# Last down block cut into 512, 448 and 128 tokens, its outputs on two queues, and two reorderings inside a streaming encoder layer

## The chip, the cores and the metric

The kernel runs on one core of one Trainium2 chip. The metric is the device time of one execution in microseconds (us). Before the change three runs took 1772.66 us in the median, from 1772.01 to 1775.33.

## The reference, cut to what matters

One encoder layer is applied to 1024 new tokens (the prompt) and to 64 tokens of a running stream (the sample), 1088 tokens of width 1024 in all. In short:

```
h = RMSNorm(x) @ W_in                      # one projection for four mixers
x = x + concat[Conv, ForgettingAttn, HGRN2, StickBreaking] @ W_out
x = x + MemoryCrossAttn(RMSNorm(x))        # 4 heads, 256 memory tokens
h = RMSNorm(x)
x = x + square(relu(h @ W_up)) @ W_down    # 1024 -> 4096 -> 1024
y = RMSNorm(x)                             # y_prompt (1024 rows), y_sample (64 rows)
```

Beside y the layer returns the new caches. Two of them are the last 30 inputs of the depthwise convolution, for the prompt and for the sample (conv_p, conv_s, each 30 x 256). Everything is float32 and must come out nearly that exact.

## The kernel before, in words

Activations lie transposed, channels on the 128 partitions and tokens along the free axis, in eight tiles of 128 channels. The tokens are in two groups (GR, L216): 512, and 576 of which the last 64 are the sample. Every dense product is made from three: each operand is split into a high half that the fast matmul takes without loss and a low rest (`split`, L169: ScalarE copies the high half, VectorE subtracts), and high x high, high x low and low x high are added up in PSUM (`mul`, L1270; `mm3`, L188). In the names of the profile `wh`, `wl` are the halves of weights, `ap`, `aq`, `fz`, `xt`, `hx` those of activations; `pw` is one PSUM bank (2 in turn), `pz` two banks (3 pairs in turn).

The program is written as a sequence of tiles and operations. A scheduler puts the operations of each engine in one fixed order ahead of time; it takes what is ready by its plan, the lower `tc.cur_priority` first. The number grows as the program is written down, and the code moves it by hand at some places. At run time each engine goes through its list in order and waits at an operation whose inputs or buffers aren't there.

Three places matter here.

First the end of the convolution (`lane_conv`, L758). It runs as one of four lanes whose work is interleaved. 31 taps for two channel tiles are VectorE's (L794). After the taps of the last chunk the two conv outputs are made (L798 to L805): for each, two transposes of 30 columns into a PSUM bank (`pco`; the pool `ps_cv` has one buffer), a copy by VectorE to `cvo` (its tag `c0` has one buffer too) and a store by SyncE (SP). The next user of `ps_cv` is the sum over channels `pme` (L811), the next of `c0` is `rs`. All lanes come ahead of the dense block of W_out that follows.

Second the first Strassen step of the up projection (loop from L1367, i = 1). The product of W_up with h is made for 2 x 2 blocks with seven products instead of eight. `forms` (L1302) makes the combinations of activations that these need: for each of four k, T1 and T2 (L1305 to L1310) and then T3 and T4 (L1311 to L1313), with their splits. It is called at L1375 inside i = 1, after 800 has been added to the priority (that stays added). `sums` (L1328) makes the combinations of weights, `wform` and `split` their halves (L1377 to L1382). TensorE then takes, for i = 1: W from the first weights (`pa`), Y from S4 and B22, Z from S2 and T2, X from S1 and T1, then onto Z again S3 with T3 and A22 with T4. The tiles wh and wl have two buffers each; those of the second weights (`pb`, S4 and A22) are the ones that the products of i = 0 used.

Third the end. The down projection goes over 8 blocks of 512 hidden channels. In the last (L1496) all weights are split first, and then the tokens are taken in parts of 512, 320 and 256: for each part and each of eight output tiles m twelve matmuls into a `pw` bank and an addition to x by VectorE (L1344, `plus`), and after the eight the part is finished:

```
def finish(g, c0, n):                  # for each 128 tokens of the part
    ps = banks()                       # 2 PSUM banks, one for each half of 1024 channels
    for kb in range(2):
        4 transposes into ps[:, kb]    # TensorE, L1467
        Square with a row sum          # ScalarE, through L74
    1/sqrt of the mean square          # six small steps of VectorE and ScalarE
    for kb: scale by it and by the gain, store   # VectorE L1472, SP L1476 or L1478
```

The last tile of tokens holds 64 rows of the prompt and 64 of the sample, so it has four stores; the others have two.

Of the kernel before, what the change touches and what calls it, by code (L numbers as in the profile page):

```python
# [8 lines left out]
F32 = mybir.dt.float32  # L9
# [3 lines left out]
AF = mybir.ActivationFunctionType  # L13
# [4 lines left out]
P = 128  # L18
D = 1024
KD = D // P  # L20
SP = 1024
# [3 lines left out]
G = 256  # L25
# [27 lines left out]
def kernel(ctx: ExitStack, tc: tile.TileContext, *args):  # L53
    nc = tc.nc
# [8 lines left out]
    y_p, y_s = y_p[0], y_s[0]  # L63
# [9 lines left out]
    def act(out, in_, func, **kw):  # L73
        nc.scalar.activation(out=out, in_=in_, func=func, **kw)  # L74

    V, Q = nc.vector, nc.gpsimd
# [4 lines left out]
    ident = const.tile([P, P], F32, name="ident")  # L81
# [28 lines left out]
    for m in LEVELS[1:]:  # L110
        nb = 64 // m
        f = const.tile([P, nb], F32, name=f"lf{m}", tag="lvlf", bufs=1)
# [56 lines left out]
    def split(hi, lo, src):  # L169
        act(hi, src, AF.Copy)  # L170
        V.tensor_tensor(out=lo, in0=src, in1=hi.bitcast(F32), op=ALU.subtract)  # L171
# [70 lines left out]
    wk = mx.enter_context(tc.tile_pool(name="wk", bufs=2))  # L242
    rb = wk.tile([P, T], F32, name="rb", tag="rb", bufs=1)
    with ExitStack() as pa:
        xa = pa.enter_context(tc.tile_pool(name="xa", bufs=1))
        ps_a = pa.enter_context(tc.tile_pool(name="ps_a", bufs=4, space=PSUM))
        ss = xa.tile([P, 9], F32, name="ss")
# [3 lines left out]
        for i, (t0, n) in enumerate(TT):  # L251
# [3 lines left out]
            if i in (3, 6):  # L255
                c = (C_SK, C_SV)[i // 3 - 1]
# [19 lines left out]
        for c0, cn in CH:  # L276
            tiles = [i for i, (t0, n) in enumerate(TT) if c0 <= t0 < c0 + cn]
            for k in range(KD):
                px = ps_a.tile([P, 512], F32, name="px", tag="px")
                for i in tiles:  # L280
                    t0, n = TT[i]
# [18 lines left out]
    ps_cv = mx.enter_context(tc.tile_pool(name="ps_cv", bufs=1, space=PSUM))  # L300
# [437 lines left out]
    HW = CW - 1  # L738
    CN = 376
    CE = SP - 2 * CN + HW + SS  # L740

    def ct_(name, tag, n=CN):
        return hc.tile([P, n], F32, name=name, tag=tag)
# [6 lines left out]
    ps = ps_cv.tile([P, 4, 64], F32, name="pcw", tag="cv")  # L750
# [7 lines left out]
    def lane_conv():  # L758
        tails = [None, None]
        for t0, np_ in ((0, CN), (CN, CN), (2 * CN, SP - 2 * CN)):  # L760
            last = t0 + np_ == SP
            n, nt = (CE, np_ + SS) if last else (np_, np_)
            ys, exts = [], []
# [32 lines left out]
                if j % 3 == 2:  # L796
                    yield 0.3 + n / 150.0
            if last:  # L798
                for at, dst in ((np_, conv_p), (CE, conv_s)):
                    ps = ps_cv.tile([P, G], F32, name="pco", tag="cv")  # L800
                    for ct in range(2):
                        nc.tensor.transpose(ps[:HW, ct * P:(ct + 1) * P], exts[ct][:, at:at + HW], ident)
                    ot = ct_("cvo", "c0")
                    V.tensor_copy(out=ot[:HW, :G], in_=ps[:HW])
                    nc.sync.dma_start(out=dst[0, 0], in_=ot[:HW, :G])  # L805
            rs = ct_("rs", "c0").rearrange("p (j n) -> p j n", j=2)
            sqs = [ct_(f"sq{ct}", f"ce{ct}", CN + HW) for ct in range(2)]
            for p0, pn in ((0, n // 2), (n // 2, n - n // 2)):
# [12 lines left out]
                v, r, t = rs[:, 0], sq[0], rs[:, 1]  # L821
# [219 lines left out]
    n = GR[0][1]  # L1041
# [222 lines left out]
    def banks():  # L1264
        return psm.tile([P, 2, 512], F32, name="pz", tag="z", bufs=3)
# [36 lines left out]
    def forms(k):  # L1302

        (h11, h12), (h21, h22) = ((xw[0][i], xw[1][i]) for i in (k, k + 4))
        V.tensor_tensor(out=h11[:, :N1], in0=h12[:, :N1], in1=h11[:, :N1], op=ALU.subtract)  # L1305
        act(h11[:, N1:], h12[:, N1:], AF.Copy)
        split(*hb[T1][k], h11)
        V.tensor_tensor(out=h12, in0=h22, in1=h12, op=ALU.subtract)
        V.tensor_tensor(out=h22, in0=h22, in1=h11, op=ALU.subtract)
        split(*hb[T2][k], h22)  # L1310
        split(*hb[T3][k], h12)  # L1311
        V.tensor_tensor(out=h21[:, :N1], in0=h21[:, :N1], in1=h22[:, :N1], op=ALU.subtract)
        split(hb[T4][k][0][:, :N1], hb[T4][k][1][:, :N1], h21[:, :N1])  # L1313
# [53 lines left out]
    for i in range(1, NU):  # L1367
        r1 = fetch_w(w_up, 0, KD, 2 * i * P)
        r2 = fetch_w(w_up, 0, KD, (2 * i + 1) * P)
        pa, pb = ([wp.tile([P, KD, P], F32R, name=nm, tag=nm) for nm in ("wh", "wl")] for _ in range(2))  # L1370
        split(*pa, r1)
        if i == 1:
            tc.cur_priority += 800
            for k in range(4):
                forms(k)  # L1375
        s1 = fz.tile([P, 4, P], F32, name="s1", tag="s1", bufs=1)
        sums(r1[:, :4], r1[:, 4:], r2[:, :4], r2[:, 4:], s1, V)  # L1377
        S2, S1 = wform(r1[:, :4]), wform(s1)
        S3 = wform(r2[:, :4])
        S4, A22 = [t[:, :4] for t in pb], [t[:, 4:] for t in pb]  # L1380
        split(*S4, r1[:, 4:])
        split(*A22, r2[:, 4:])  # L1382
        t1 = t1s[i % 2]
        W, Z, X = bank(), banks(), banks()
        mul(W, [t[:, :4] for t in pa], hb[B11], True, slice(0, N1))
        act(t1[:, :N1], W, AF.Copy)
        c12, c22 = unit("ap"), unit("ap")
        if i == 1:

            mul(W, [t[:, 4:] for t in pa], hb[B21], False, slice(0, N1))  # L1390
            Y = banks()
            mul2(Y, S4, hb[B22], True)
            plus(halves(c12), halves(t1), Y[:, :, :HN])
        mul2(Z, S2, hb[T2], True)
        plus(halves(c12), halves(c12 if i == 1 else t1), Z[:, :, :HN])
        mul2(X, S1, hb[T1], True)
        plus(halves(c22), halves(t1), X[:, :, :HN])
        if i == 1:
            plus(halves(c12), halves(c12), X[:, :, :HN])
        else:  # L1400
            mul(W, [t[:, 4:] for t in pa], hb[B21], False, slice(0, N1))
        c11 = unit("xt")
        square(c11[:, :N1], W)
        mul2(Z, S3, hb[T3], False)
        plus(halves(c22), halves(c22), Z[:, :, :HN])
        square(c22, c22, q)
        if i > 1:
            mul2(X, S4, hb[B22], False)
            plus(halves(c12), halves(c12), X[:, :, :HN])
        square(c12, c12, q)  # L1410
        mul2(Z, A22, hb[T4], False, N1)
        c21 = unit("xt")
        plus(c21[:, :HN], t1[:, :HN], Z[:, 0, :HN])
        plus(c21[:, HN:N1], t1[:, HN:N1], Z[:, 1, :N1 - HN])
        square(c21[:, :N1], c21[:, :N1])
        store_hidden(i, (c11, c12, c21, c22))
# [39 lines left out]
    def finish(g, c0, n):  # L1456

        for i in range(0, n, P):
            w = min(P, n - i)
            t = GR[g][0] + c0 + i  # L1460
            np_ = max(0, min(w, SP - t))
            ss = fs.tile([P, 2], F32, name="fss", tag="fss")
            ps = banks()
            yt = [unit("aq") for _ in range(2)]
            for kb in range(2):
                for k in range(4):
                    nc.tensor.transpose(ps[:w, kb, k * P:(k + 1) * P], xT[g][4 * kb + k][:, c0 + i:c0 + i + w], ident)  # L1467
                act(yt[kb][:w, :512], ps[:w, kb], AF.Square, accum_out=ss[:w, kb:kb + 1])
            V.tensor_tensor(out=ss[:w, 0:1], in0=ss[:w, 0:1], in1=ss[:w, 1:2], op=ALU.add)
            r = rstd_chain(fs, 1, ss[:w, 0:1], "rf", scale=1.0 / D, parts=w)  # L1470
            for kb in range(2):
                V.scalar_tensor_tensor(out=yt[kb][:w, :512], in0=ps[:w, kb], scalar=r, in1=gf[kb][:w],  # L1472
                                       op0=ALU.mult, op1=ALU.mult)
                ys = slice(kb * 512, (kb + 1) * 512)
                if np_:
                    nc.sync.dma_start(out=y_p[t:t + np_, ys], in_=yt[kb][:np_, :512])  # L1476
                if np_ < w:
                    nc.sync.dma_start(out=y_s[t + np_ - SP:t + w - SP, ys], in_=yt[kb][np_:w, :512])  # L1478

    for c in range(NC):  # L1480
        hid = hidden(c)
        if c == 0:
            for k in range(KD):
                for g, (t0, n, _) in enumerate(GR):
                    nc.sync.dma_start(out=xT[g][k], in_=x2_d[k][:, t0:t0 + n])
        if c < NC - 1:
            for j in range(KD // 2):
                for m, w in enumerate(down_w(c, j, None)):
                    ps = bank()
                    mul(ps, w, [hid[k][0] for k in range(NF)], True, slice(0, N1))  # L1490
                    plus(xT[0][2 * j + m], xT[0][2 * j + m], ps)
                    ps = banks()
                    mul2(ps, w, [hid[k][1] for k in range(NF)], True)
                    x = halves(xT[1][2 * j + m])
                    plus(x, x, ps[:, :, :HN])
        else:  # L1496

            ws = []
            for j in range(KD // 2):
                dst = [[t[:, :NF * P].rearrange("p (k c) -> p k c", k=NF) for t in pair(1 - c % 2)] for m in range(2)]  # L1500
                ws += down_w(c, j, dst)
            for g, c0, n in ((0, 0, 512), (1, 0, 320), (1, 320, 256)):
                for m in range(KD):
                    ps = bank()[:, :n]
                    mul(ps, ws[m], [hid[k][g] for k in range(NF)], True, slice(c0, c0 + n))
                    x = xT[g][m][:, c0:c0 + n]
                    plus(x, x, ps)
                finish(g, c0, n)
# [33 lines left out]
```

## Time and profile before

| | |
|---|---|
| runs before, median of 3 | 1772.66 us (1772.01 to 1775.33) |
| profiled execution | 1772.62 us, its span 1770.6 us, mean granted TensorE clock 0.987 |
| TensorE matmul (PE) busy | 1698.2 us, 96% |
| weight load (PEld) busy | 1506.6 us, 85% |
| VectorE (DVE) busy | 1174.6 us, 66% |
| ScalarE (ACT) busy | 791.5 us, 45% |
| GpSimd (POOL) busy | 93.6 us, 5% |

Shares are means over the whole span. A busy TensorE is not yet one at its peak, since matmuls overlap. All dense products stand at line L71, all ScalarE operations at L74 and the low halves of all splits at L171, since helpers record them; they are told apart by the names of the tiles.

### The profile page before, as it was taken

To read this page: it belongs to the slowest core of one execution; us is meant where nothing else is said; L and a number is where in the kernel's file an instruction comes from. 1 tells how busy PE (TensorE), PEld (TensorE's weight loads), DVE (VectorE), ACT (ScalarE), POOL (GpSimd) and SP (SyncE) were. 2 spreads that over 40 slices of the span, in tenths; PEclk is the share of its full clock that TensorE was granted. 3 is DMA by queue.
4 is the path that set the end of the run, shared out by engine and by line. 5 is a ranking of instruction groups with operands and counts; after the bars stand their busy time and mean duration, and the time that the engine had idled before them with its cause. 6 is when DMAs were issued, how large, how long until landed. Compare 5 with 4: busy or idle time off the path is not lost.

```text
span 1770.6 us, 29390 instructions
## 1 busy us (share of the span) xinstructions
PE 1698.2 (96%) x11379; PEld 1506.6 (85%) x11379; DVE 1174.6 (66%) x2231; ACT 791.5 (45%) x1614; POOL 93.6 (5%) x201
## 2 busy tenths in 40 slices
PE   6999999999999979999999989999999999999997
PEld 4987768788777768988899979999999999999987
DVE  6366789988986897668777795555555444444435
ACT  5266657647356755346456353343334212122213
POOL 3021201101020100000000000000000000000000
PEclk9999999999999989999999999999999999999999
DMA  8521322243237357222522323333335732332112
GB/s 255 144 76 44 111 78 84 80 113 88 63 99 215 101 155 233 81 88 68 158 78 72 118 91 107 99 99 103 101 100 194 272 98 87 98 99 73 36 36 102
DMA packets 233195, 194.70 MB, mean 110 GB/s; under 512 B 17502, under 2 KB 199711, under 8 KB 233055
## 3 DMA queue, kind: packets, MB, share of 16 engines
q1 hardware_dynamic: 232799, 192.80, 35.5%
q8 instruction: 90, 1.47, 0.4%
q14 instruction: 50, 0.41, 0.1%
q0 software_dynamic: 256, 0.01, 0.0%
HBM read 137.96 MB, written 53.72 MB: 108 GB/s over the span
## 4 chain that ended last, share of the span: by engine, by line
PE 78%; DVE 13%; ACT 4%; DMA 2%; issue 2%; POOL 0%; SPq 0%; DVEq 0%; POOLq 0%; ACTq 0%
PE pz L71 25%; PE pw L71 16%; PE pm L71 11%; PE pa L71 9%; PE pq L71 5%; PE z L71 2%; DVE y L794 2%; PE pmo L71 2%; PE pms L71 1%; PE po L71 1%; PE pt L517 1%; PE pv L71 1%; DVE hsc L933 1%; DVE sba L494 1%; DVE wl L171 1%
## 5 line engine op out<-in xcount | busy, mean ns | idle before, releaser
L74 ACT ACTIVATE wh<-wr 128x1024 fp32r<-128x1024 f32 (+1 forms) x179 | 161.5, 910 | 446.6 <-PE pz L71 193.8
L171 DVE TENSOR_TENSOR wl<-wr,wh 128x1024 fp32r<-128x1024 f32 (+1 forms) x179 | 184.5, 1037 | 68.8 <-ACT wh L74 67.6
L71 PE MATMUL pw<-ap,wh 128*128 128x512 f32 x720 | 223.4, 391 | 1.3 <-ACT t L74 0.7
L71 PE MATMUL pz<-ap,wh 128*128 128x288 f32 x988 | 198.3, 294 | 0.0
L71 PE MATMUL pa<-ap,wh 128*128 128x256 f32 (+2 forms) x768 | 187.1, 332 | 2.2 <-DVE xt L1119 2.2
L71 PE MATMUL pm<-hx,wh 128*128 128x512 f32 (+1 forms) x640 | 176.4, 364 | 1.9 <-ACT wh L74 1.7
L71 PEld LDWEIGHTS pz<-ap,wh 128*128 128x128 f32 x988 | 161.3, 188 | 4.7
L71 PE MATMUL pm<-ap,wh 128*128 128x256 f32 (+1 forms) x768 | 164.7, 308 | 0.0
L71 PEld LDWEIGHTS pw<-ap,wh 128*128 128x128 f32 x720 | 130.1, 188 | 24.1 <-ACT t L74 1.1
L71 PE MATMUL pz<-ap,wl 128*128 128x288 f32 x494 | 145.5, 294 | 0.0
L71 PEld LDWEIGHTS pa<-ap,wh 128*128 128x128 f32 x768 | 131.7, 190 | 12.6 <-DVE xt L1119 2.4
L71 PE MATMUL pw<-ap,wl 128*128 128x512 f32 x360 | 140.4, 390 | 0.0
L71 PE MATMUL pa<-ap,wl 128*128 128x512 f32 (+2 forms) x384 | 126.8, 331 | 1.1 <-DVE wl L171 1.1
L71 PEld LDWEIGHTS pm<-hx,wh 128*128 128x128 f32 x640 | 110.5, 192 | 20.3 <-ACT wh L74 2.5
L71 PEld LDWEIGHTS pm<-ap,wh 128*128 128x128 f32 x768 | 123.9, 191 | 4.2 <-issue 1.7
L1344 DVE TENSOR_TENSOR xt<-xt,pz 128x576 f32<-128x576 f32 x56 | 42.2, 754 | 113.8 <-PE pz L71 108.5
L71 PE MATMUL pm<-ap,wl 128*128 128x256 f32 (+1 forms) x384 | 114.2, 297 | 0.0
L71 PE MATMUL pm<-hx,wl 128*128 128x512 f32 (+1 forms) x320 | 112.9, 353 | 0.3 <-DVE wl L171 0.2
L794 DVE SCALAR_TENSOR_TENSOR y<-ext,cwT,y 128x376 f32<-128x376 f32 (+1 forms) x180 | 101.1, 609 | 0.3
L1344 DVE TENSOR_TENSOR xt<-xt,pw 128x512 f32<-128x512 f32 (+2 forms) x80 | 51.1, 639 | 69.6 <-PE pw L71 69.6
L71 PE MATMUL pq<-ap,wh 128*128 128x512 f32 (+2 forms) x384 | 93.1, 332 | 0.0
L71 PEld LDWEIGHTS pz<-ap,wl 128*128 128x128 f32 x494 | 92.7, 188 | 0.0
(380 smaller groups left out, 3580.7 us busy)
## 6 DMA issues: line engine op xcount, KB each, us to landing
wr<-in_w_up_dram SPq DMA_DIRECT2D x32, 512.0 KB, 4.0
wr<-in_w_down_dram SPq DMA_DIRECT2D x32, 512.0 KB, 3.5
wr<-in_w_in_dram SPq DMA_DIRECT2D x24, 512.0 KB, 4.3
hid_d<-ap SPq DMA_DIRECT2D x32, 288.0 KB, 2.5
aq<-hid_d SPq DMA_DIRECT2D x32, 288.0 KB, 3.2
wr<-in_w_out_dram SPq DMA_DIRECT2D x16, 512.0 KB, 3.5
wr<-in_w_mq_dram SPq DMA_DIRECT2D x16, 512.0 KB, 3.7
wr<-in_w_mo_dram SPq DMA_DIRECT2D x32, 256.0 KB, 2.7
```

The costliest lines, as they stand in the source:

```text
L71: nc.tensor.matmul(out, lhsT=lhsT, rhs=rhs, start=start, stop=stop, **kw)
L74: nc.scalar.activation(out=out, in_=in_, func=func, **kw)
L171: V.tensor_tensor(out=lo, in0=src, in1=hi.bitcast(F32), op=ALU.subtract)
L494: V.tensor_tensor_scan(out=v[:, ::-1], data0=z[:, n - 1:0:-1], data1=v[:, ::-1], initial=-NEG, op0=ALU.add, op1=ALU.subtract)
L517: nc.tensor.transpose(ps[:w, j - jb], p[:, j * P:j * P + w], ident)
L794: V.scalar_tensor_tensor(out=y, in0=ext[:, j:j + n], scalar=cwT[:, ct, j:j + 1], in1=y, op0=ALU.mult, op1=ALU.add)
L933: V.copy_predicated(sc[r, s_at:s_at + ng, :, r].rearrange("p g h (c w) -> p (g h) c w", w=2 * m)[:, :, :, m:], lvl[m][r, par * nb:(par + 1 ...
L1344: eng.tensor_tensor(out=out, in0=a, in1=b, op=ALU.add)
```

## The change

The conv outputs get one PSUM tile with room for both. All four transposes come first, then one copy of 512 columns into a tile of another pool (tag `nat`, two buffers), then the two stores.

`forms` is cut in two, T1 and T2 in the first, T3 and T4 in the second (`forms2`). The call, with the 800 on the priority, moves behind the sums and splits of the weights of i = 1, and runs the first for all four k and then the second for all four.

In the last block the parts are 512, 448 and 128 tokens. For the part of 128 the two halves of the channels are transposed into two pairs of banks, of which each uses one bank; the other parts keep one pair. The stores of y_sample go out from ScalarE's queue.

```diff
             if last:
-                for at, dst in ((np_, conv_p), (CE, conv_s)):
-                    ps = ps_cv.tile([P, G], F32, name="pco", tag="cv")
+                ps = ps_cv.tile([P, 2, G], F32, name="pco", tag="cv")
+                for o, at in enumerate((np_, CE)):
                     for ct in range(2):
-                        nc.tensor.transpose(ps[:HW, ct * P:(ct + 1) * P], exts[ct][:, at:at + HW], ident)
-                    ot = ct_("cvo", "c0")
-                    V.tensor_copy(out=ot[:HW, :G], in_=ps[:HW])
-                    nc.sync.dma_start(out=dst[0, 0], in_=ot[:HW, :G])
+                        nc.tensor.transpose(ps[:HW, o, ct * P:(ct + 1) * P], exts[ct][:, at:at + HW], ident)
+                ot = wk.tile([P, 512], F32, name="cvo", tag="nat").rearrange("p (o c) -> p o c", o=2)
+                V.tensor_copy(out=ot[:HW], in_=ps[:HW])
+                for o, dst in enumerate((conv_p, conv_s)):
+                    nc.sync.dma_start(out=dst[0, 0], in_=ot[:HW, o])
...
         split(*hb[T2][k], h22)
+
+    def forms2(k):
+
+        (h11, h12), (h21, h22) = ((xw[0][i], xw[1][i]) for i in (k, k + 4))
         split(*hb[T3][k], h12)
...
         split(*pa, r1)
-        if i == 1:
-            tc.cur_priority += 800
-            for k in range(4):
-                forms(k)
         s1 = fz.tile([P, 4, P], F32, name="s1", tag="s1", bufs=1)
         sums(r1[:, :4], r1[:, 4:], r2[:, :4], r2[:, 4:], s1, V)
...
         split(*A22, r2[:, 4:])
+        if i == 1:
+            tc.cur_priority += 800
+            for f in (forms, forms2):
+                for k in range(4):
+                    f(k)
...
-            ps = banks()
+            if n > P:
+                ps = banks()
+                ps = [ps[:, kb] for kb in range(2)]
+            else:
+                ps = [banks()[:, 0] for kb in range(2)]
...
                 if np_ < w:
-                    nc.sync.dma_start(out=y_s[t + np_ - SP:t + w - SP, ys], in_=yt[kb][np_:w, :512])
+                    nc.scalar.dma_start(out=y_s[t + np_ - SP:t + w - SP, ys], in_=yt[kb][np_:w, :512])
...
-            for g, c0, n in ((0, 0, 512), (1, 0, 320), (1, 320, 256)):
+            for g, c0, n in ((0, 0, 512), (1, 0, 448), (1, 448, 128)):
```

## Rows read from the trace of the kernel before

**Rows 1.** Busy us of each engine (x instructions) by stretch, granted clock, DMA.

```profile
640.00:657.40 17.40, 6.76 (x63) 5.11 (x61) 17.40 (x35) 5.01 (x10) 0.00 (x0) 0.76 0.41 133
...
1020.00:1046.00 26.00, 25.36 (x153) 22.94 (x152) 25.93 (x42) 15.54 (x26) 0.00 (x0) 1.00 0.30 96
1046.00:1058.30 12.30, 5.84 (x25) 4.16 (x23) 12.26 (x21) 8.37 (x16) 0.00 (x0) 0.88 0.12 45
1058.30:1073.10 14.80, 14.74 (x96) 14.39 (x97) 9.91 (x15) 3.46 (x6) 0.00 (x0) 0.87 0.27 72
...
1743.70:1758.30 14.60, 14.60 (x123) 14.14 (x122) 9.07 (x29) 5.58 (x20) 0.00 (x0) 1.00 0.27 91
1758.30:1770.60 12.30, 1.73 (x13) 1.05 (x10) 4.73 (x15) 2.65 (x10) 0.00 (x0) 0.65 0.30 85
```

**Rows 2.** Timeline of TensorE around i = 1: start, length, operation [wait, releaser].

```profile
1045.92 0.62 PE L71 MATMUL pw<-ap,wh 128*128 128x512 f32 x2
...
1058.31 0.85 PE L71 MATMUL pz<-fz,wh 128*128 128x288 f32 x2 [5.78 <-ACT wh L74]
...
1062.49 0.43 PE L71 MATMUL pz<-fz,wh 128*128 128x288 f32 x2
...
1062.89 0.43 PE L71 MATMUL pz<-fz,wh 128*128 128x288 f32 x2
```

**Rows 3.** Timeline of VectorE and ScalarE from 1055 us.

```profile
1055.10 0.69 DVE L171 TENSOR_TENSOR xt<-xt 128x512 fp32r<-128x512 f32 x1
...
1056.90 0.69 DVE L1333 TENSOR_TENSOR wr<-wr 128x512 f32<-128x512 f32 x1
...
1057.63 0.63 ACT L74 ACTIVATE wh<-wr 128x512 fp32r<-128x512 f32 x1
...
1059.31 0.69 DVE L171 TENSOR_TENSOR ap<-wr,ap 128x512 fp32r<-128x512 f32 x1
```

**Rows 4.** VectorE's groups by shape, 1026 to 1060 us: busy us, mean ns.

```profile
L1312 DVE TENSOR_TENSOR xt<-xt 128x512 f32<-128x512 f32 x4 | 2.8, 690 | 0.0
L171 DVE TENSOR_TENSOR xt<-xt 128x576 fp32r<-128x576 f32 x3 | 2.3, 755 | 0.0
...
L171 DVE TENSOR_TENSOR xt<-xt 128x512 fp32r<-128x512 f32 x3 | 2.1, 691 | 0.0
```

**Rows 5.** Timeline at the end of the convolution.

```profile
655.68 0.61 PE L802 MATMUL pco<-ident,ext 128*30 128x128 f32 x2 [8.62 <-DVE cvo L804]
...
657.42 0.80 PE L71 MATMUL pa<-ap,wl 128*128 128x512 f32 x1 [1.12 <-DVE wl L171]
...
660.57 1.42 PE L71 MATMUL pme<-y,ones 128*128 128x183 f32 x4
```

**Rows 6.** The chain that ended last, in the last block: start, length, what.

```profile
1703.05 21.89 PE pw L71 x96
...
1736.66 7.08 PE pw L71 x48
...
1755.44 2.88 PE pw L71 x24
```

**Rows 7.** Timeline of TensorE at matmuls of 64 columns.

```profile
941.42 0.28 PE L71 MATMUL pmo<-pT,vl 128*128 128x64 f32 x1
...
942.31 0.28 PE L71 MATMUL pmo<-pT,vl 128*128 128x64 f32 x1
```

**Rows 8.** Timeline of the last two tiles of tokens.

```profile
1758.83 0.31 PEld L1467 LDWEIGHTS pz<-ident,xt 128*128 128x128 f32 x3 [0.20 <-DVE xt L1344]
...
1760.51 0.66 PE L1467 MATMUL pz<-ident,xt 128*128 128x128 f32 x4 [1.14 <-ACT aq L74]
...
1761.47 1.41 DVE L1472 SCALAR_TENSOR_TENSOR aq<-pz,rsy,gf 128x512 f32<-128x512 f32 x2
...
1764.28 1.41 DVE L1472 SCALAR_TENSOR_TENSOR aq<-pz,rsy,gf 128x512 f32<-128x512 f32 x2
...
1766.87 0.59 SPq L1478 DMA_DIRECT2D out_dram<-aq  x1
```

More of the change, by code (lines that the diff above doesn't have):

```diff
@@ L1466, in finish @@
                 for k in range(4):
-                    nc.tensor.transpose(ps[:w, kb, k * P:(k + 1) * P], xT[g][4 * kb + k][:, c0 + i:c0 + i + w], ident)
-                act(yt[kb][:w, :512], ps[:w, kb], AF.Square, accum_out=ss[:w, kb:kb + 1])
+                    nc.tensor.transpose(ps[kb][:w, k * P:(k + 1) * P], xT[g][4 * kb + k][:, c0 + i:c0 + i + w], ident)
+                act(yt[kb][:w, :512], ps[kb][:w], AF.Square, accum_out=ss[:w, kb:kb + 1])
             V.tensor_tensor(out=ss[:w, 0:1], in0=ss[:w, 0:1], in1=ss[:w, 1:2], op=ALU.add)
@@ L1471, in finish @@
             for kb in range(2):
-                V.scalar_tensor_tensor(out=yt[kb][:w, :512], in0=ps[:w, kb], scalar=r, in1=gf[kb][:w],
+                V.scalar_tensor_tensor(out=yt[kb][:w, :512], in0=ps[kb][:w], scalar=r, in1=gf[kb][:w],
                                        op0=ALU.mult, op1=ALU.mult)
```

## The prediction

> **What bounds the kernel now.** I read the stretches first [rows 1]. TensorE is the bound almost everywhere, and it stands idle in three places that the diff touches. Between 640 and 657.4 us it is busy 6.76 of 17.40 us while VectorE is busy for all 17.40. Between 1046 and 1058.3 us it is busy 5.84 of 12.30 us, VectorE 12.26. After 1758.3 us only 1.73 of 12.30 us are left to it: the tail of the last tiles. In both holes VectorE is the engine that ends last; in the tail it is a chain from one token tile to the next. TensorE's clock pays for the holes: it is granted 0.76 in the first, 0.88 in the second and 0.87 in the stretch behind it, and 1.00 where the products flow.
>
> Then the timeline at the second hole [rows 2]. W begins at 1045.92, its last product ends near 1052.3 us, and the product Y (S4 times B22, matmuls pz<-fz,wh) starts at 1058.31 after 5.78 us of waiting for ACT wh, the high half of S4. The other two engines say why [rows 3]: ScalarE writes this wh at 1057.63, directly behind VectorE's L1333 (the last step of `sums`), and that stands at 1056.90 because the whole of `forms` for four k, whose last split is at 1055.10, has been put ahead of it. T3 and T4, which `forms` also makes there, are wanted only two and three products after Y.
>
> **The change part by part.**
>
> *Order at i = 1 (sums before forms, forms in two passes).* No instruction is added or dropped. The weight chain (four subtractions, five splits, some 0.6 us each on VectorE, 5.4 us in all) no longer queues behind `forms`; what it waits for is its inputs. S4 uses the second pair of wh and wl tiles, which the two Z products of i = 0 hold until TensorE passes from them to W at 1045.92. So S4 can be split from 1046 on and is there by about 1049, three microseconds before TensorE comes for it. TensorE then goes from W to Y at 1052.3: 6.0 us earlier [rows 2].
>
> What is late next is T1 and T2, then T3. VectorE is full from 1026 to 1060.0, where the last split of the weights ends [rows 3]. The second pass takes out the T3 split, L1312 and the T4 split for four k: 2.3 + 0.75 + 2.8 + four of 0.69 = 8.6 us of busy time [rows 4], 7.5 us when the 0.09 by which neighbours overlap (from 1055.10 to 1056.90 three of 0.69 start 0.60 apart [rows 3]) is taken off twelve times. So T1, T2 and all weights are done by 1060.0 - 7.5 = 1052.5, in time for Z at 1055.5 (Y is 24 matmuls of 288 columns, 3.2 us). The second pass ends at 1060.0. Behind it stand the additions c12 = t1 + Y and c12 + Z (0.67 us each), and S3 times T3 is accumulated onto the Z that the second one reads: 1061.4, where TensorE arrives at 1061.9. The cover is thin, and the weights of i = 2 come from the same queue, so I charge 0.8 us for it.
>
> The clock comes on top: the 96 matmuls from 1058.31 to 1073.1 took 14.8 us at a granted 0.87 [rows 1]. From 1062.49 on three take 0.40 us, 0.132 each [rows 2]; 96 of these are 12.7 us. Without the idle stretch that is 2.1 us less. Together -6.0 - 2.1 + 0.8 = **-7.3 us**. Bounds: -8.1 where VectorE costs nothing; 0 where the chain cannot move (the third rival). Behind this place TensorE has no idle time of note up to the last block, so the gain stays.
>
> *The conv outputs.* Before, two pairs of transposes share one bank in turn, so the second pair waits for the first copy, which VectorE does after all taps: 8.62 us of TensorE time [rows 5]. After, four transposes go early and one copy of 512 columns follows the taps. But the next thing TensorE needs is VectorE's wl, also behind the taps; TensorE waited another 1.12 us for it and started at 657.42 [rows 5]. So most of the 8.62 us is not to be had. One copy instead of two has twice the columns ahead of that wl: +0.3 us. Against it, the first four pme matmuls, now at 660.57 [rows 5] in the stream of the dense block, can run while TensorE waits, since their bank is free after the single copy: -1.2 us. The wait for the landing of the first output, in which the second copy could not start, goes too; only the conv chain stands behind it, and what that makes is read for the second token group, behind the first one's 192 products of 0.228 us, 44 us. Bounds: -3.5 (six more products of high halves, 512 columns each and so 0.43 us at the 1.2 GHz level, also move into the hole) to +1.5 (conv's vector work, set free earlier, gets ahead of the splits). The row nearest is the wl that TensorE waits for; I take **-0.8 us**. SP only loses a wait: the same two stores leave, back to back.
>
> *The last block: 512, 448, 128.* Columns and matmuls stay (1088 columns, 288 matmuls); their cost per matmul does not. The chain has 96 of 512 columns in 21.89 us (228 ns), 48 of 320 in 7.08 us (147.5 ns), 24 of 256 in 2.88 us (120 ns) [rows 6]. A 448 is 147.5 + 128 x 80.5/192 = 201 ns, so the second part costs 19.3 us instead of 14.2: +5.1. For 128 columns no row exists. A straight line gives 65 ns; but matmuls of 64 columns follow each other every 111 ns (eight intervals from 941.42 to 942.31 [rows 7]), so something that does not depend on the columns, the weight load in front of every one, sets a floor. 128 lies under it: 111 ns, 10.7 us against 11.5, only -0.9 where the line gives -5.3. Bounds 65 and 120 ns, 6.2 and 11.5 us.
>
> The Trainium skill has another number: "TensorE: Matmul & The Clock Gate", Back-to-back issue gap, gives about 81 ns for a sustained stream of weight load and matmul at N = 128. By it this part would be an estimated 7.8 us, 2.9 less. The trace's 111 ns disagrees for these weights, and I go by the trace.
>
> One tile more is transposed ahead of the last product (its neighbour had stood behind it): 8 at 0.115 us, (14.6 - 11.5)/27 from the third part's 123 matmuls [rows 1], +0.9. So the last product ends 5.1 - 0.9 + 0.9 = 5.1 us later, near 1763.4.
>
> Behind it there is one tile instead of two. Before, from 1758.3 to the end of the last scaling, 1764.28 + 1.41 = 1765.7 [rows 8], is 7.4 us; the second tile's last transposes waited for the Square of its own first half (1760.51, behind ACT), which two places remove. The first tile alone: addition until 1758.8, last transpose, scaling done at 1761.47 + 1.41 = 1762.9: 4.6, with a 128-column addition 4.4 us. That is -3.0. The stores: SP issued four, 0.55 to 0.59 us each, the last at 1766.87 [rows 8]. On two queues the last one starts with the end of the scaling: -1.2 us. No row shows an issue on ScalarE's queue; it is bounded by SP's 0.59 from below and, should it be dear, by +1 us; nothing is queued behind it there. Sum +5.1 - 3.0 - 1.2 = **+0.9 us**, between -3.5 (65 ns) and +3 (VectorE's scalings, 1.41 us a tile, hold a bank longer than the 1.33 us of twelve matmuls).
>
> Sum: -7.3 - 0.8 + 0.9 = -7.2 us. The profiled execution took 1772.62 us (span 1770.6 and 2.0 around it), as good as the median of 1772.66. **1765.4 us.**
>
> **The rivals.**
>
> *VectorE's debt comes back, 1769.3.* VectorE has done nothing less by 1060.0. If TensorE, past Y, must wait with Z until the queue is through, only Y (3.2 us) and some of the clock (1 us) are gained, and -7.3 becomes about -3.4. For: VectorE is full for 34 us, and the margin for T3 is half a microsecond. Against: what is moved back is not needed until the third product.
>
> *The clock falls in the last part: slower, 1775.* One mechanism: the part of 128 columns is short products with 36 transposes among them. If that brings the 1.2 GHz level, as the idle stretch up to 1058.3 us did, the 10.7 + 4.1 us can take twice as long. The kernel is slower once more than 7.2 us are lost, about half of that stretch; two thirds lost are 10, 1765.4 + 10 = 1775. Against: the third part with 27 transposes has 1.00 [rows 1].
>
> *The reorder does not bite, 1772.7.* If the weight chain still cannot start (its tiles share buffers with those that i = 0 holds), TensorE waits as before: 0 - 0.8 + 0.9. Against: ScalarE's wh follows L1333 at once, so no buffer was what it waited for.
>
> *The short product is cheaper than the floor, 1763.2.* If more of the weight load hides behind 128 moving columns than behind 64, halfway between the line and the floor, 88 ns, the part takes 8.4 us and the sum falls by 2.2. For: the 64-column rows are ten matmuls in another stage. Against: the 256 of the same block stand only 9 ns above the floor, as if they already met it. By the 81 ns that the Trainium skill's page "TensorE: Matmul & The Clock Gate" states it would be an estimated 1762.5.
>
> **How the numbers follow.** Forecast 0.60, debt 0.20, clock 0.05, no bite 0.10, cheap product 0.05. The forecast's own range is 1762 to 1768.5. A measurement tells 0.2%, 3.5 us, from no change. Faster: 0.58 of the forecast, half of the debt, the cheap product, 0.73; same: 0.02, the other half, most of no bite, 0.19; slower: the clock and the rest, 0.08. The range, 1761.0 to 1772.8, leaves out the clock, the far end of the cheap product and some of no bite.
>
> **What would show it.** Y follows W with under 1 us of waiting, the granted clock is near 1.00 from 1046 to 1073, and T4's split stands behind the weights' splits. At 655 us no wait for cvo, but one for wl. In the last part, twelve matmuls in 1.33 us; one tile behind the last product; the last two stores start together. I am wrong if TensorE waits for a T form, if the 128-column matmuls come at another spacing, or if the last block saves over 2 us.

## The result: 4.7% slower, and the two traces beside each other

The changed kernel takes 1858.0 us (median of four runs, 1852.2 to 1858.5; before beside it 1772.3 us). The ratio is 1.0472, with a 95% interval of 1.0448 to 1.0496. The prediction, 1765.4 us and 1772.8 at the upper end, is wrong in sign and in size. The profiled execution took 1858.3 us with a span of 1856.6 us, 86.0 us more than before.

Three landmarks of TensorE that exist in both traces divide these 86.0 us: the first matmul of W at i = 1, the first of the last block, and the end of the span. Until W it is 1127.40 instead of 1045.92 us, **+81.5**. From there to the last block it is 1776.56 - 1127.40 = 649.2 instead of 1702.89 - 1045.92 = 657.0 us, **-7.8**. The last block and the tail take 1856.6 - 1776.56 = 80.0 instead of 1770.6 - 1702.89 = 67.7 us, **+12.3**. (The chain in [rows 6] counts the block from 1703.05; here both starts are those of TensorE's timeline. The expectations of the experiments have 657.1, 67.5 and so -8.0 and +12.5.) The second Strassen step gave what was forecast. The other two places did not.

The first products of the last block in that timeline, before:

```profile
1702.89 22.05 PE L71 MATMUL pw<-ap 128*128 128x512 f32 x96
```

and in the changed kernel:

```profile
1776.56 22.02 PE L71 MATMUL pw<-ap 128*128 128x512 f32 x96
```

**The 81.5 us.** Before, between 500 and 600 us TensorE is busy for nine tenths of the time. Busy us (x instructions) of TensorE, its weight loads, VectorE, ScalarE and GpSimd, granted clock, DMA share and GB/s:

```profile
500.00:600.00 100.00, 90.38 (x725) 75.41 (x724) 78.11 (x185) 68.52 (x186) 22.41 (x34) 0.95 0.50 143
600.00:660.00 60.00, 49.34 (x406) 41.33 (x407) 56.03 (x110) 34.06 (x68) 0.00 (x0) 0.91 0.45 134
```

The same view of the changed kernel has 261 matmuls instead of 725 there, at half the clock:

```profile
500.00:600.00 100.00, 49.41 (x261) 29.44 (x261) 72.93 (x177) 32.48 (x93) 25.45 (x34) 0.52 0.11 32
600.00:660.00 60.00, 43.49 (x258) 39.04 (x259) 33.23 (x80) 20.88 (x58) 0.00 (x0) 0.80 0.43 113
660.00:740.00 80.00, 76.06 (x634) 67.28 (x640) 42.56 (x72) 62.48 (x135) 0.00 (x0) 1.00 0.60 176
```

VectorE is about as busy as before and ScalarE less than half, so no engine has become the bound. What is missing is work for TensorE: the projections. Their natural-order copies (`nat<-pn`, ScalarE, from a PSUM bank of the projections to a tile of tag `nat`, then a store) show where they stopped. Timeline of ScalarE before (start, length, operation, [wait, releaser]), two of the last three:

```profile
478.60 0.60 ACT L74 ACTIVATE nat<-pn 128x512 f32<-128x512 f32 x1 [2.39 <-PE pn L365]
...
492.90 0.38 ACT L74 ACTIVATE nat<-pn 128x256 f32<-128x256 f32 x1 [1.72 <-PE pn L365]
```

and all three in the changed kernel:

```profile
587.65 0.45 ACT L74 ACTIVATE rsy<-rsy 128x320 f32<-128x320 f32 x1
588.01 0.58 ACT L74 ACTIVATE nat<-pn 128x512 f32<-128x512 f32 x1
595.12 0.38 ACT L74 ACTIVATE nat<-pn 128x256 f32<-128x256 f32 x1 [6.54 <-DMA out_dram<-nat]
612.21 0.38 ACT L74 ACTIVATE nat<-pn 128x256 f32<-128x256 f32 x1 [16.70 <-DMA out_dram<-cvo]
```

The two buffers of `nat` can be followed in these rows. The first copy has one of them; the second waits 6.54 us for the first one's store, so it is in the same buffer; the third waits 16.70 us for the store of cvo, which holds the other. TensorE had transposed into the first pn bank at 493.42. It goes on with projections only when the copy has emptied that bank, and meanwhile works at what the other lanes leave it (timeline of TensorE):

```profile
493.42 0.38 PE L365 MATMUL pn<-ident,kT 128*128 128x128 f32 x2
...
588.64 1.22 PE L71 MATMUL pm<-hx,wh 128*128 128x512 f32 x2 [2.33 <-ACT nat L74]
...
610.26 1.59 PE L71 MATMUL pme<-y,ones 128*128 128x183 f32 x4 [14.15 <-DVE cvo L804]
```

The last row is the end of the convolution, which stands in [rows 5] at 660.57. VectorE's taps run to 609.53, the one copy to cvo is 0.67 us, and its two stores leave SP back to back at 610.23. So the conv lane itself was 50 us earlier than before, while the lane that feeds TensorE was held back. Behind the projections everything is late: the 16 copies of the memory's keys and values run from 652.0 to 733.1 instead of 547.0 to 644.0 us, and the first product of W_out comes at 736.93 instead of 645.86.

The waits that name a buffer are 6.54 and 16.70 us. The larger part, from 493.8 to 588.01 us, shows no such wait: the first copy stands directly behind another lane's `rsy` in ScalarE's fixed order, so its place in that order is what held it, and why the plan put it there isn't seen in the trace.

**The second Strassen step** [rows 1 to 3]. W has 24 products. In the changed kernel Y (pz<-fz,wh) starts without a wait behind the first twelve of them; then, after 0.60 us for ScalarE's copy to t1, come the other twelve and the rest of Y. Before, TensorE had waited 0.69 us at the same point of W and 5.78 us ahead of Y. Timeline of TensorE in the changed kernel:

```profile
1127.40 0.62 PE L71 MATMUL pw<-ap,wh 128*128 128x512 f32 x2
...
1129.91 0.39 PE L71 MATMUL pw<-ap,wl 128*128 128x512 f32 x1
1130.14 0.42 PE L71 MATMUL pz<-fz,wh 128*128 128x288 f32 x2
...
1132.62 0.76 PE L71 MATMUL pw<-ap,wh 128*128 128x512 f32 x2 [0.60 <-ACT t L74]
...
1135.53 0.29 PE L71 MATMUL pz<-fz,wh 128*128 128x288 f32 x1
```

W and Y together take 9.60 us (1127.40 to 1137.00) instead of 17.77 (1045.92 to 1063.69). The row of the shorter wait before:

```profile
1049.51 0.73 PE L71 MATMUL pw<-ap,wh 128*128 128x512 f32 x2 [0.69 <-ACT t L74]
```

In the changed kernel, the stretches that answer to 1046 to 1073 us have TensorE busy 12.00 of 12.60 us and a clock of 1.00 where it had been 0.88 and 0.87:

```profile
1127.40:1140.00 12.60, 12.00 (x73) 10.72 (x72) 12.60 (x22) 9.43 (x16) 0.00 (x0) 1.00 0.44 131
1140.00:1154.90 14.90, 14.90 (x106) 14.07 (x105) 14.60 (x24) 7.73 (x14) 0.00 (x0) 1.00 0.15 57
```

**The last block** [rows 6, 8]. Timeline of TensorE in the part of 128 columns (x counts instructions that follow each other):

```profile
1822.39 2.14 PE L1477 MATMUL pz<-ident,xt 128*128 128x128 f32 x16
1824.28 0.87 PE L71 MATMUL pw<-ap 128*128 128x128 f32 x6
1825.78 0.66 PE L1477 MATMUL pz<-ident,xt 128*128 128x128 f32 x4 [0.62 <-ACT aq L74]
...
1827.79 1.11 PE L1477 MATMUL pz<-ident,xt 128*128 128x128 f32 x8 [0.74 <-ACT aq L74]
...
1829.88 0.63 PE L1477 MATMUL pz<-ident,xt 128*64 128x128 f32 x4 [0.48 <-ACT aq L74]
1830.26 2.32 PE L71 MATMUL pw<-ap 128*128 128x128 f32 x19
1833.83 1.56 PE L71 MATMUL pw<-ap 128*128 128x128 f32 x12 [1.24 <-DVE xt L1349]
1836.29 10.50 PE L71 MATMUL pw<-ap 128*128 128x128 f32 x48 [0.90 <-DVE xt L1349]
```

Five waits, 3.98 us in all: three for ScalarE's Squares of the four tiles of 448, two for additions (L1349) that stand on VectorE behind the scalings of these tiles, 1.41 us each. Then the 48 matmuls at the end take 10.50 us, 219 ns each, and the stretches say at which clock:

```profile
1825.00:1830.00 5.00, 3.16 (x26) 2.67 (x26) 2.89 (x13) 3.80 (x17) 0.00 (x0) 1.00 0.27 105
1830.00:1833.00 3.00, 2.58 (x23) 2.44 (x22) 2.94 (x11) 0.90 (x4) 0.00 (x0) 1.00 0.27 104
1833.00:1836.00 3.00, 1.56 (x12) 1.42 (x12) 2.59 (x9) 0.41 (x2) 0.00 (x0) 0.98 0.64 245
1836.00:1840.00 4.00, 3.71 (x18) 3.71 (x18) 0.72 (x4) 0.00 (x0) 0.00 (x0) 0.50 0.28 66
1840.00:1847.00 7.00, 7.00 (x34) 7.00 (x34) 0.75 (x3) 0.00 (x0) 0.00 (x0) 0.50 0.01 2
```

0.50 is 1.2 GHz; it begins behind the stretch from 1825 to 1836 us, in which TensorE was busy for 7.30 of 11 us, and it stays at 0.50 through 7.00 us in which TensorE is busy all the time.

### The profile page after: what moved, and what is told of

Its sections match the earlier page's. It is cut to its first block, busy times and chain, and to the rows that moved or that the text cites. A ratio compares the mean times of both kernels' runs of the same rounds, so it can differ in the third digit from the quotient of the medians.

```text
span 1856.6 us, 29416 instructions
## 1 busy us (share of the span) xinstructions
PE 1729.8 (93%) x11366; PEld 1527.3 (82%) x11379; DVE 1176.7 (63%) x2230; ACT 792.3 (43%) x1614; POOL 96.3 (5%) x201
## 5 line engine op out<-in xcount | busy, mean ns | idle before, releaser
L1349 DVE TENSOR_TENSOR xt<-xt,pz 128x576 f32<-128x576 f32 x56 | 42.2, 753 | 113.8 <-PE pz L71 109.1
L1349 DVE TENSOR_TENSOR xt<-xt,pw 128x512 f32<-128x512 f32 (+2 forms) x80 | 51.0, 638 | 80.7 <-PE pw L71 80.5
```

Of the source, the lines that this page charges most:

```text
L1349: eng.tensor_tensor(out=out, in0=a, in1=b, op=ALU.add)
```

## The experiments

Theory A: the 81.5 us come from the place of `cvo` in tag `nat`, and the last block costs its 12.3 us by itself. Rival B lays the first on the single PSUM bank. Times of before differ by chip (medians 1773.7, 1774.8, 1775.2 us in the three groups), so each kernel is compared with the runs of before beside it, and stages between landmarks of one trace. In the cuts of code "..." stands for lines left out.

**e1, the outputs back in the conv lane's own tag.** One bank stays.

```diff
-                ot = wk.tile([P, 512], F32, name="cvo", tag="nat").rearrange("p (o c) -> p o c", o=2)
-                V.tensor_copy(out=ot[:HW], in_=ps[:HW])
                 for o, dst in enumerate((conv_p, conv_s)):
-                    nc.sync.dma_start(out=dst[0, 0], in_=ot[:HW, o])
+                    ot = ct_("cvo", "c0")
+                    V.tensor_copy(out=ot[:HW, :G], in_=ps[:HW, o])
+                    nc.sync.dma_start(out=dst[0, 0], in_=ot[:HW, :G])
```

> The changed kernel with one edit: the conv outputs keep the one PSUM tile with all four transposes ahead, but go out through two copies in the conv lane's own tag c0 instead of one copy in tag nat. Theory A (cvo stands in the hand-out order of the two nat buffers ahead of the copies of fox's last K, and holds the projections back): the 81.5 us by which the first product of the up block's W came later are gone, and the time is 1772.3 - 8.0 (second Strassen step) + 12.5 (last block) = about 1777 us, 1773 to 1781. Rival B (the one PSUM bank, taken by all four transposes until the taps are through, holds the next sums of the convolution back and with them the stage): it stays at about 1858 us.

Measured 1778.0 us, ratio to before 1.0022 (1.0008 to 1.0037). The 81 us are gone with the tag, so B falls. The timeline also shows what the outputs are worth without the accident. TensorE has no wait for cvo any more, and the same time goes into a wait for wl:

```profile
650.43 1.20 PE L71 MATMUL pa<-ap,wh 128*128 128x512 f32 x4
...
662.14 0.79 PE L71 MATMUL pa<-ap,wl 128*128 128x512 f32 x1 [10.51 <-DVE wl L171]
```

From the first of these products to this one it is 11.71 us, before 11.56 (645.86 to 657.42 [rows 5]).

**e2, the tag alone, in the kernel before.**

```diff
-                    ot = ct_("cvo", "c0")
+                    ot = wk.tile([P, 512], F32, name="cvo", tag="nat")
```

> The kernel before with one edit: its two cvo tiles come from tag nat instead of tag c0; banks, copies and order stay as they were. Theory A: the projections stall as in the changed kernel, 1772.3 + 81 = about 1853 us, or more, since two tiles now stand in the hand-out (1840 to 1880). Rival B (the bank): nothing of note changes, 1768 to 1777 us.

Measured 1854.0 us, ratio 1.0445 (1.0418 to 1.0471). One line costs 80 us. Here cvo takes two tiles of the tag, and the first natural copy waits for one of their stores directly (ScalarE's timeline):

```profile
608.86 0.60 ACT L74 ACTIVATE nat<-pn 128x512 f32<-128x512 f32 x1 [23.37 <-DMA out_dram<-cvo]
```

**e3, the reorderings at i = 1 alone** (forms in two passes, behind the sums and splits).

```diff
...
-        if i == 1:
-            tc.cur_priority += 800
-            for k in range(4):
-                forms(k)
...
+        if i == 1:
+            tc.cur_priority += 800
+            for f in (forms, forms2):
+                for k in range(4):
+                    f(k)
```

> The kernel before with the two reorderings at i = 1 alone (sums and splits ahead, forms in two passes). Theory A: from the first matmul of W at i = 1 to the last down block the changed kernel takes 649.2 us where the one before took 657.1, so alone it gives 1772.3 - 8.0 = 1764.3 us, 1763 to 1766. Rival C (part of the 8.0 us came from weights that had arrived long before because the mixers were late): -4 us or less, 1768 us or more.

Measured 1764.8 us against 1773.7 beside it, ratio 0.9942 (0.9920 to 0.9965). In its trace it is 1763.2 - 1046.36 = 716.8 us from W to the end, before 1770.6 - 1045.92 = 724.7: -7.8. Rival C falls.

**e4, the last block alone** (parts, two places, two queues).

```diff
...
-            for g, c0, n in ((0, 0, 512), (1, 0, 320), (1, 320, 256)):
+            for g, c0, n in ((0, 0, 512), (1, 0, 448), (1, 448, 128)):
```

> The kernel before with the last block alone changed (512, 448, 128, two places, two queues). Theory A: the last block by itself costs the 12.5 us that the two traces show from its first matmul on (80.0 instead of 67.5 us): 1784.8 us, 1782 to 1788, with 48 matmuls of 128 columns at a granted clock of 0.50. Rival D (the low clock is left over from the long slow stage of the mixers, or from another place, and not made by this block): clock 1.00 there, 48 matmuls in 5.3 instead of 10.5 us, about 1778 us or less.

Measured 1786.4 us, ratio 1.0067 (1.0044 to 1.0089), 12.7 us above the median of before. The low clock is there without any slow mixer stage, for 60 matmuls now, so D falls:

```profile
1764.03 13.06 PE L71 MATMUL pw<-ap 128*128 128x128 f32 x60 [1.25 <-DVE xt L1344]
```

e3 and e4 add up to -8.9 + 12.7 = +3.8 us; e1, which has both and the single bank, has +4.3.

**e5, only the tail of the change, on the old parts** (with the reorderings of e3). The y_sample stores go out from ScalarE's queue as in the change, and the last tile alone has two places:

```diff
...
-            ps = banks()
+            if g == 0 or c0 + i + P < GR[1][1]:
+                ps = banks()
+                ps = [ps[:, kb] for kb in range(2)]
+            else:
+                ps = [banks()[:, 0] for kb in range(2)]
...
```

> Both reorderings at i = 1, the parts of before (512, 320, 256), and from the last block only the two queues for outputs and two places for the very last tile of tokens. Theory A (behind the last product a tile's chain and the issue of stores set the end): the second tile's last transposes no longer wait for its own first Square, its scalings start with the end of the first tile's, 1.4 us earlier, and the last store starts 1.2 us earlier, so 1764.8 - 2.6 = 1762.2 us, 1761 to 1763.5. Rival E (the scalings of the tile ahead or the issue on ScalarE take the place of what goes): 1764 us or more.

Measured 1763.2 us, ratio 0.9934 (0.9920 to 0.9948). The interval overlaps that of e3, so the times don't tell the two apart. In the traces, from the transposes behind the last product to the end it is 1762.1 - 1751.01 = 11.1 us, in e3 1763.2 - 1750.73 = 12.5: 1.4 us of the 2.6 expected. In VectorE's timeline the last scalings start at 1756.72, 5.7 us behind the last product, and in e3 6.1 us (1756.86). So two places gave 0.4 of the 1.4 us priced, since the small steps of the second tile's root still stand behind the first tile's scalings:

```profile
1754.75 1.41 DVE L1481 SCALAR_TENSOR_TENSOR aq<-pz,rsy,gf 128x512 f32<-128x512 f32 x2
1756.08 0.15 DVE L152 TENSOR_TENSOR rst<-rsy 128x1 f32<-128x1 f32 x1
...
1756.72 1.41 DVE L1481 SCALAR_TENSOR_TENSOR aq<-pz,rsy,gf 128x512 f32<-128x512 f32 x2
```

**e6, the tiles of 448 finished behind all products.**

```diff
...
-                finish(g, c0, n)
+                if (g, c0) != (1, 0):
+                    if c0:
+                        finish(1, 0, 448)
+                    finish(g, c0, n)
```

> The kernel before with the last block of the change, but the part of 448 is finished (transposed, scaled, stored) only behind all products of the part of 128, so that TensorE finds neither transposes nor full VectorE queues among these products. Theory F (the low clock comes from the stalls, TensorE being busy 8.3 of 14 us while VectorE finishes the four tiles of 448): the 96 matmuls of 128 columns run at a granted clock of 1.00, 111 ns each, 10.7 us in all. Theory G (short products alone bring the low clock): 0.50 sets in among them all the same, and the second half takes 219 ns each. The end is late in either case, since five tiles stand behind the last product: about 1785 us by F, 1790 by G.

Measured 1782.0 us, ratio 1.0051 (1.0036 to 1.0066). The 96 matmuls of 448 and the 96 of 128 columns now follow each other, and the clock stays up through all of them:

```profile
1748.00:1751.00 3.00, 3.00 (x29) 2.98 (x27) 0.94 (x3) 0.00 (x0) 0.00 (x0) 1.00 0.00 0
1751.00:1758.60 7.60, 7.60 (x71) 7.60 (x70) 1.70 (x6) 0.00 (x0) 0.00 (x0) 1.00 0.00 0
```

VectorE's additions, one behind every twelve products, give the price of a product:

```profile
1745.87 0.62 DVE L1344 TENSOR_TENSOR xt<-xt,pw 128x448 f32<-128x448 f32 x1 [1.86 <-PE pw L71]
1748.35 0.62 DVE L1344 TENSOR_TENSOR xt<-xt,pw 128x448 f32<-128x448 f32 x1 [1.86 <-PE pw L71]
...
1756.33 0.29 DVE L1344 TENSOR_TENSOR xt<-xt,pw 128x128 f32<-128x128 f32 x1 [1.05 <-PE pw L71]
1757.67 0.29 DVE L1344 TENSOR_TENSOR xt<-xt,pw 128x128 f32<-128x128 f32 x1 [1.05 <-PE pw L71]
```

2.48 / 12 = 207 ns for 448 columns and 1.34 / 12 = 112 ns for 128, the floor taken from [rows 7]. Short products alone don't bring the low clock: G falls. (The end came 3 us earlier than expected. The trace of the changed kernel has TensorE busy for 10.3 of 14 us from 1822 to 1836, where the expectation says 8.3.)

**e7, one pair of banks for the last tile too.**

```diff
-            if n > P:
+            if n > 0:
```

> The kernel before with the last block of the change, but with one pair of banks for both halves of the last tile too (no second place); parts of 512, 448, 128 and two queues stay. Theory A (the parts cause the loss, the second place only helps the tail): 48 matmuls at 0.50 as before, and the end 0 to 1.5 us later than the 1786.4 us with two places: 1786 to 1788. Rival H (the pair of banks taken early by the second place is missing for the tiles of 448 and makes TensorE's waits): the 4.9 us of waits go, and the clock with them: 1776 us or less.

Measured 1785.8 us, ratio 1.0073 (1.0057 to 1.0088), 0.2 us under A's range and far above H's, with nothing to see of the second place in the time. TensorE's waits and the low clock are as in the changed kernel, so H falls:

```profile
1759.89 1.55 PE L71 MATMUL pw<-ap 128*128 128x128 f32 x12 [1.25 <-DVE xt L1344]
1762.35 10.50 PE L71 MATMUL pw<-ap 128*128 128x128 f32 x48 [0.91 <-DVE xt L1344]
```

**e8, cvo in `nat`, but written down behind the projections.** The changed kernel; the projections' lane says when all of it is written, and the conv lane waits for that before its outputs.

```diff
...
+        done.add("projected")
...
             if last:
+                yield Need("projected")
                 ps = ps_cv.tile([P, 2, G], F32, name="pco", tag="cv")
```

> The changed kernel with one edit: the convolution's lane waits, while the program is written down, until the projections are all written, before it writes its outputs; cvo stays one tile of tag nat, one copy, one bank. Theory A (what costs the 81.5 us is the place of cvo in the order in which the two nat buffers are handed out, ahead of the copies of fox's last K): these copies go ahead of it again and the time is that of e1, about 1777 us, 1774 to 1781. Rival I (a store's buffer in tag nat, or the single copy of 512 columns behind the taps, is itself what costs): 1840 us or more.

Measured 1778.9 us, ratio 1.0013 (1.0001 to 1.0025). Tag, copy, bank and stores are those of the changed kernel; only the place in the sequence in which the program is written differs (theirs, and that of what the conv lane writes behind them), and the 81 us are gone. The three natural copies are back at 481 to 495 us. Rival I falls. ScalarE's last natural copy:

```profile
495.13 0.39 ACT L74 ACTIVATE nat<-pn 128x256 f32<-128x256 f32 x1 [1.72 <-PE pn L365]
```

and TensorE at the end of the convolution. Here the pme sums do move ahead of the wl, as the prediction had it, but the wait for cvo in front of them is as long as the one it replaces:

```profile
657.36 1.59 PE L71 MATMUL pme<-y,ones 128*128 128x183 f32 x4 [9.05 <-DVE cvo L806]
659.09 0.79 PE L71 MATMUL pa<-ap,wl 128*128 128x512 f32 x1
```

**e9, the tiles of 448 finished one by one among the products of 128.**

```diff
...
+                    if c0 == 448 and m % 2:
+                        t0 = m // 2 * P
+                        finish(1, t0, min(P, 448 - t0))
-                finish(g, c0, n)
+                if (g, c0) != (1, 0):
+                    finish(g, c0, n)
```

> The kernel before with the last block of the change, but the four tiles of the part of 448 are finished one by one, behind the second, fourth, sixth and eighth output tile of the part of 128, instead of all at its start. Theory F (stalls bring the waits and the low clock; the products themselves are priced rightly at +5.1 us): the granted clock stays at 1.00 through the 128-column products, the last block takes 67.5 + 5.1 - 2.5 (tail) = about 70 us instead of 79 to 80, 1776 us in all. Rival G (transposes among short products bring the low clock by themselves): 0.50 sets in again, 1784 us or more.

Measured 1780.0 us, ratio 1.0027 (1.0014 to 1.0040). The clock is 1.00 through the products, with the transposes among them, so F holds and the second G falls:

```profile
1757.00:1762.00 5.00, 4.64 (x42) 4.50 (x42) 3.09 (x13) 1.99 (x7) 0.00 (x0) 1.00 0.27 105
1762.00:1766.00 4.00, 3.65 (x34) 3.50 (x33) 2.42 (x10) 1.78 (x6) 0.00 (x0) 1.00 0.34 131
```

Its size was missed: block and tail take 1778.5 - 1705.20 = 73.3 us, not 70. The products end at 1765.84, +5.4 us against before (60.6 instead of 55.3). But the last tile of 448 is finished behind the last product, together with that of 128, and the 12.7 us of tail have nothing left of the saving. So even spread out, the parts of 448 and 128 cost 4.9 us against those of before.

**e10, what is left that is good.** The reorderings, the tail of e5 and the conv outputs as in e8; it has no edit of its own.

> Both reorderings at i = 1, the parts of before with two queues and two places for the last tile (as e5), and the conv outputs through one bank and one copy to nat, written behind the projections (as e8). Theory A (conv outputs are worth nothing, since the wl behind the taps is what TensorE waits for in any case): the time of e5, 1763.2 us, 1761.5 to 1765. Rival J (the first row of the prediction's -0.8 holds: sums of the convolution move into the hole): 1762 us or less.

Measured 1763.4 us, ratio 0.9925 (0.9905 to 0.9945): e5's time, above J's bound, so no gain of the conv part shows. A gain of 0.8 us can't be ruled out by these times, whose intervals are 5 to 7 us wide. The stage itself, from the first product of W_out to the first for the second token group, takes 58.6 us in e8 and 59.0 in e10, against 59.0 to 59.9 in the seven kernels with the old order of the conv outputs. e3, e5 and e10 all beat both kernels, before by 0.6 to 0.8%; the reordering at i = 1 is what they have in common.

## Why the prediction was wrong

*The conv outputs, "-0.8 us", "-3.5 [...] to +1.5": this step failed, by 82 us.* It priced what the instructions of the place do: transposes, one copy, a wait of SP. The sentence "SP only loses a wait" treats cvo as an end of the work. The diff also moved cvo to a tag that another lane needs, and the text before the prediction even gives its two buffers. What was not asked: who takes the next buffers of this tag, and where do these stand in the written program? cvo is written down ahead of the natural copies of the last projections, and its store stands behind all 31 taps. e2 shows that the tag alone costs it, e8 that its place in the written order does. How the scheduler's plan comes to set the first of the three copies as late as 588.01, where no wait for a buffer shows, is not read from these traces; nor was `nat` with three buffers tried.

The mechanism that *was* argued there was half right. That "most of the 8.62 us is not to be had", because wl follows at once, is what e1 shows, more strictly than priced: 11.71 us against 11.56. The -1.2 for the sums moved into the hole came in e8 with a wait of its own. So apart from the tag no run shows a gain of this term; the -0.8 itself is too small for these runs to tell from 0.

*Order at i = 1, "-7.3 us": right.* -7.8 in the changed kernel and in e3. The wait ahead of Y is gone and the clock is 1.00, the two terms of the sum; of the 0.8 charged for VectorE's queue 0.3 came. One step went another way: the prediction has Y behind all of W, and S4 was there in time for Y to start behind W's first half, which is where the plan now puts it. The rivals "debt" and "does not bite" fall.

*The last block, "+0.9 us": wrong by 11.4.* The sizes of the products hold: priced were 201 and 111 ns, measured 207 and 112 (e6), which makes +5.8 us instead of +5.1. What failed is that the order around them was taken as free. The prediction saw the collision and gave it away as a bound: "VectorE's scalings, 1.41 us a tile, hold a bank longer than the 1.33 us of twelve matmuls", up to +3 in all. The part of 128 begins with four tiles to be finished where its model, the part of 256, has three, in 10.7 us of products. That made 4.0 us of waits and, through them, the 1.2 GHz level: 48 x (219 - 112) = 5.1 us. The tail gave -2.5 of the -4.2 expected (9.8 us behind the last product instead of 12.3); its eight transposes at half speed are 0.8 of the difference (1.74 us instead of 8 x 0.115). Another 0.6 is the last store: from the start of its issue to the end of the span it is 4.3 us on ScalarE's queue (1851.55 + 0.71 to 1856.6) and 3.7 before on SP's (1766.87 to 1770.6), where the prediction put the two alike. The other 0.3 stays open. 5.8 + 4.0 + 5.1 - 2.5 = 12.4 us, with 12.3 seen. The rival "the clock falls" had chance 0.05 and the wrong trigger: it argued from short products with transposes among them, which e9 shows at 1.00 (and e6 without the transposes). The stalls are what differs; finishing the same tiles spread out (e9) keeps the clock.

The Trainium skill's "TensorE: Matmul & The Clock Gate", Back-to-back issue gap, has about 81 ns for N = 128. This case's traces don't agree: e6 measures 112 at the full clock. So going by the trace was right here, and the rival of the cheap product falls.

## What to carry to other kernels

When an edit moves a tile to another tag or pool, list who takes that tag's next buffers in the order in which the program is written, and when the new tile is released; a buffer that is released late, written ahead of an urgent lane, can hold that lane back by far more than its own work takes (80 us here). When a product is cut smaller, compare what must be finished during it (per tile, on the slowest helper) with its length, and spread that work, since a stall costs twice where the clock falls behind it: 4.0 us of waits and 5.1 us of slow products here. 

## What the runs showed of the hardware

- The floor of a short product follows the clock: 112 ns at 1.00 (e6) and 219 ns at 0.50 for the same 128 columns.
- An issue on ScalarE's queue takes 0.71 us (1.42 us for two), beside 0.56 on SP (1.12 for two):

```profile
1851.55 1.12 SPq L1486 DMA_DIRECT2D out_dram<-aq  x2
1851.55 1.42 ACTq L1488 DMA_DIRECT2D out_dram<-aq  x2
```

- Where the mixers' code is the same, the first product of W_out comes at 644.29 (e3), 645.66 (e9), 645.86 (before) or 649.14 us (e4): a run's start of a later stage says little, its length much.
